# Softmax(scores) @ v on one core: dropping the own-engine waits of the exps and of the copies of transposed tiles

## The chip, the cores and the metric

The kernel runs on one core of one Trainium2 chip. The metric is device time in microseconds (us), taken as the median of several executions of a kernel. Times of profiled executions ("spans") are quoted beside it where a trace is read; they are a little shorter than the measured time.

A core has separate engines that run their own instruction streams: TensorE (PE for its matmuls, PEld for its weight loads), VectorE (DVE), ScalarE (ACT), GpSimd (POOL) and SyncE (SP), and DMA queues that move data. They tell each other of progress through semaphores: counters that instructions step up when they finish, and that other instructions wait on.

## The reference, cut to what matters

```python
scores: (8, 12, 1024, 1024) float32      # 96 heads, 402 MB
v:      (8, 12, 1024, 64)   float32
attn = exp(scores - max)                 # row by row
attn = attn / (sum(attn) + 1e-8)
out  = attn @ v                          # (8, 12, 1024, 64) float32
```

## The kernel before

Four heads are worked on in one iteration of a hardware loop of 24 iterations. One head has R = 8 "rows"; here a row is a tile of 128 rows of scores, 128x1024. For each row ScalarE computes exp into fp16 (mostly two rows in one instruction), TensorE transposes it in C = 8 pieces of 128x128 into PSUM, VectorE copies the transposed row to SBUF, and, two rows later (LAG = 2), TensorE multiplies it with v in 8 matmuls. v has a column of ones, so that the row sums come along. At the end of a head VectorE takes reciprocals and multiplies (`normalise`). The kernel takes exp of the scores as they are: it neither subtracts the maximum nor adds 1e-8.

```python
def heads(n0):
    for k in range(AHEAD):                        # AHEAD = 4 heads
        ...
        for r in range(R):
            if r % EB == 0:                       # EB = 2
                p_nat = take(p_bufs)              # 8 buffers, in turn
                ...
                    nc.scalar.activation(out=p_nat[...], in_=s_bufs[k][...], func=EXP)   # cut
            p_row = p_nat[:, r % EB, :].rearrange(...)
            psT = take(psT_bufs)                  # 4 buffers
            for c in range(C):
                nc.tensor.transpose(out=psT[:, c*P:(c+1)*P], in_=p_row[...], identity=order16[:])
            pt = take(pt_bufs)                    # 4 buffers
            copy = nc.vector.tensor_copy(out=pt[:], in_=psT[:])
            ...
            pending.append((n0, k, r, pt, st))
            if len(pending) > LAG:
                finish(pending.pop(0))            # 8 product matmuls that read pt
    while pending:
        finish(pending.pop(0))
    last(n0)                                      # loads and stores of the iteration's end
...
with tc.For_i(0, BH, AHEAD, iteration_sync="reg_based") as n0:
    queued.clear()
    heads(n0)
```

The framework orders every access to a buffer by semaphores. A copy into `pt` waits for PE, since the product that read the buffer's old content must be done and the new transposes must have landed. It also waits on VectorE's own counter, since the same buffer was written by VectorE four copies earlier. The same holds for an exp, with ScalarE's own counter.

The softmax here doesn't subtract the row's maximum and nothing guards it: scores larger than these inputs give would overflow.

Of the kernel before, what the change touches and what calls it, by code (L numbers as in the profile page):

```python
# [14 lines left out]
def kernel(  # L15
# [6 lines left out]
    nc = tc.nc  # L22
# [69 lines left out]
    def take(bufs):  # L92
        k = turn.get(id(bufs), 0)
        turn[id(bufs)] = k + 1
        return bufs[k % len(bufs)]
# [22 lines left out]
    def normalise(k, st, first, last, behind=None):  # L118

        psO = psO_whole if k % 2 == 0 else psO_banks[first]  # L120
        psO = psO[:, :, 0 : G * M].rearrange("p b (g m) -> p b g m", m=M)
        recip = st["recip"][:, first:last]
        inverse = nc.vector.reciprocal(out=recip, in_=psO[:, :, :, D : D + 1])  # L123
        if behind is not None:
            after(inverse, behind)
        h = k % T
        for t in range(T):
            part = slice(t * W, (t + 1) * W)
            rows = st["out_sb"][h * W : (h + 1) * W, t, first * G : last * G, :]
            nc.vector.tensor_tensor(  # L130
                out=rows.rearrange("j (b g) d -> j b g d", g=G),
                in0=psO[part, :, :, 0:D],
                in1=recip[part].to_broadcast([W, last - first, G, D]),
                op=mybir.AluOpType.mult,
            )

    def finish(u):

        n0, k, r, pt, st = u
        b, g = r // G, r % G  # L140
        if r == 0:
            st["recip"] = take(rc_bufs)
            st["out_sb"] = out_bufs[k // T]
        bank = psO_whole[:, b] if k % 2 == 0 else psO_banks[b][:, 0]
        for c in range(C):
            nc.tensor.matmul(  # L146
                out=bank[:, g * M : (g + 1) * M],
                lhsT=pt[:, c * P : (c + 1) * P],
                rhs=st["vones"][:, c, 0:M],
                start=(c == 0),  # L150
                stop=(c == C - 1),
            )
        if k % 2 == 1:
            if g == G - 1 and (b > 0 or k < AHEAD - 1):
                normalise(k, st, b, b + 1)
        elif r == R - 1:
            normalise(k, st, 0, R // G)
        if r == R - 1:
            spread_v(k)
            if k == T - 1:  # L160
                store(n0, 0)

    def store(n0, k, parts=1):

        rows = out_bh.rearrange("(m x) y -> m x y", x=P)
        size = T * R * D // parts
        for part in range(0, T * R * D, size):
            dma = nc.sync.dma_start(
                out=rows[bass.ds((n0 + k) // T, 1)].rearrange("o x y -> (o x) y")[
                    :, part : part + size  # L170
                ],
                in_=out_bufs[k // T][:].rearrange("x t r d -> x (t r d)")[:, part : part + size],
            )
            for other in stores:
                apart(dma, other)
                apart(other, dma)
            apart(dma, dma)
            stores.append(dma)
            queue(dma)

    stores = []

    def apart(dma, other):
        tc.declare_no_dep(
            dma.ins, other.ins, across_iterations=True, reason="stores of two heads are disjoint"
        )

    def load(k, n, parts=(R,), r=0, **cond):
        for rows in parts:
# [29 lines left out]
    def load_next(k, n0):  # L219

        if k < AHEAD - 2:
            load(k, (n0 + (AHEAD + k)) % BH, cond=n0 < BH - AHEAD)

    def last(n0):


        before = queued[-1:]

        with tc.If(n0 < BH - 2 * AHEAD) as cmp:  # L229
            queued[:] = before  # L230
            load(AHEAD - 2, (n0 + (2 * AHEAD - 2)) % BH)
            load_v((n0 + 2 * AHEAD) % BH)
            load(AHEAD - 1, (n0 + (2 * AHEAD - 1)) % BH)
            store(n0, AHEAD - T)
        with cmp.Else():
            with tc.If(n0 < BH - AHEAD) as cmp2:
                queued[:] = before
                load(AHEAD - 2, BH - 2, (4, 4))
                load(AHEAD - 1, BH - 1, (3,))
                store(n0, AHEAD - T)  # L240
                load(AHEAD - 1, BH - 1, (2, 1, 1, 1), 3)
            with cmp2.Else():
                queued[:] = before
                store(n0, AHEAD - T, T)

    def heads(n0):

        for k in range(AHEAD):
            st = dict(vones=vones_bufs[k])
            for r in range(R):  # L250
                if r % EB == 0:
                    p_nat = take(p_bufs)
                    rows = 1 if k == AHEAD - 1 and r > 0 else EB
                    for g in range(0, EB, rows):
                        nc.scalar.activation(  # L255
                            out=p_nat[:, g : g + rows, :].rearrange(
                                "p r (x v) -> p x r v", v=Q * L
                            ),
                            in_=s_bufs[k][:, r + g : r + g + rows, :].rearrange(
                                "p r (i x l) -> p x (r i) l", i=Q, l=L  # L260
                            ),
                            func=EXP,
                        )
                p_row = p_nat[:, r % EB, :].rearrange("p (h q l) -> p h l q", q=P, l=L)
                psT = take(psT_bufs)
                for c in range(C):
                    nc.tensor.transpose(  # L267
                        out=psT[:, c * P : (c + 1) * P],
                        in_=p_row[:, c // L, c % L, :],
                        identity=order16[:],  # L270
                    )
                pt = take(pt_bufs)
                copy = nc.vector.tensor_copy(out=pt[:], in_=psT[:])  # L273
                if k == AHEAD - 1 and r == R - 1:

                    normalise(k, st, 0, 1, copy)
                if r == R - 1:
                    load_next(k, n0)
# [5 lines that stand above are left out]
        last(n0)  # L284
# [8 lines left out]
# [3 lines that stand above are left out]
# [30 lines left out]
```

## Time and profile before

| | before |
|---|---|
| time, median of three runs | 1063.8 us (1063.76 to 1064.1) |
| profiled span | 1062.3 us |
| instructions | 33,094 |
| busiest engine | ACT, 70% of the span |
| DMA | share of 1.00 in every full loop period, some 432 GB/s |
| after the last landing of scores (1052.0 us) | 10.2 us |

The table says that the kernel is bound by its transfers: no engine is busy all the time, the DMA queues are. Only the last 10 us, in which the last rows are computed and stored, depend on the engines. The lines behind this stand in the prediction below. Two more lines matter for what follows, groups of the page (line, engine, operation, output and input with shapes, count; then busy us and mean ns of one; then the engine's idle time before them and what ended most of it); L255 are the exps, L273 the copies (the transposes are L267, the product is L146).

```profile
L255 ACT ACTIVATE p_nat<-s_nat 128x2048 f16<-128x2048 f32 (+1 forms) x456 | 709.4, 1630 | 219.1 <-DMA s_nat<-in_scores_dram 192.3
...
L273 DVE COPY pt<-psT 128x1024 f16<-128x1024 f16 x768 | 518.1, 689 | 367.1 <-PE L146 134.9
```

VectorE idles 367 us before its copies, and what ended this idle time is PE, not VectorE.

### The profile page before, as it was taken

How to read it: one execution, taken by the hardware profiler on the slowest of the kernel's cores; microseconds unless marked ns; L12 is line 12 of the kernel's file. 1: busy time of each engine (PE TensorE's matmuls, PEld its weight loads, DVE VectorE, ACT ScalarE, POOL GpSimd, SP SyncE). 2: the span in 40 equal slices, each digit the busy share in tenths (PEclk: the TensorE clock that was granted, in tenths of full speed). 3: DMA queues.
4: the chain of work that ended last, by engine and by line, in shares of the span. 5: the costliest groups of instructions: out<-in, count | busy, mean ns of one | idle time of the engine just before them, and what ended most of it. 6: DMA issues, size and time to landing. Idle time of an engine off the chain costs nothing.

```text
span 1062.3 us, 33094 instructions
## 1 busy us (share of the span) xinstructions
PE 722.0 (68%) x12288; PEld 676.5 (64%) x12288; DVE 679.9 (64%) x1205; ACT 740.1 (70%) x480; POOL 243.5 (23%) x406
## 2 busy tenths in 40 slices
PE   2765766767766767667576776767677686666776
PEld 2755756666655667666576666766566676665765
DVE  1765756757666666666676666767567576676667
ACT  3766776666767668676685866767666677666686
POOL 3113112131121311212112221132121311203113
PEclk9988888879898787887988878889888788899889
DMA  9999999999999999999999999999999999999996
GB/s 397 430 417 434 428 434 434 432 435 428 434 432 432 427 433 435 434 434 427 433 429 435 428 433 435 426 441 431 431 434 429 430 428 438 434 434 432 426 432 260
DMA packets 25059, 453.05 MB, mean 426 GB/s; under 512 B 2784, under 2 KB 2784, under 8 KB 9440
## 3 DMA queue, kind: packets, MB, share of 16 engines
q1 hardware_dynamic: 25056, 453.00, 99.4%
q8 instruction: 3, 0.05, 0.0%
HBM read 436.21 MB, written 25.17 MB: 434 GB/s over the span
## 4 chain that ended last, share of the span: by engine, by line
DMA 62%; PE 12%; PEld 6%; DVE 5%; ACT 5%; issue 3%; POOL 3%; SPq 1%; POOLq 1%; ACTq 0%; DVEq 0%; PEldq 0%
DMA s_nat<-in_scores_dram 62%; PE psT L267 7%; DVE pt L273 5%; ACT p_nat L255 5%; PE psO L146 3%; POOL vones L212 3%; PEld L267 3%; PEld L146 3%; PE psO_whole L146 1%; SPq L203 1%; SPq L191 0%; POOLq L212 0%; POOLq L229 0%; POOLq L293 0%; POOLq L321 0%
## 5 line engine op out<-in xcount | busy, mean ns | idle before, releaser
L255 ACT ACTIVATE p_nat<-s_nat 128x2048 f16<-128x2048 f32 (+1 forms) x456 | 709.4, 1630 | 219.1 <-DMA s_nat<-in_scores_dram 192.3
L267 PE MATMUL psT<-order,p_nat 128*128 128x128 f16 x6144 | 562.8, 246 | 281.3 <-ACT p_nat L255 280.9
L273 DVE COPY pt<-psT 128x1024 f16<-128x1024 f16 x768 | 518.1, 689 | 367.1 <-PE L146 134.9
L267 PEld LDWEIGHTS <-p_nat 128*128 128x128 f16 x6144 | 445.4, 123 | 303.5 <-ACT p_nat L255 300.8
L212 POOL CAST vones<-v_sb 32x512 f16<-32x512 f32 x400 | 242.8, 607 | 815.3 <-PE L267 440.3
L146 PEld LDWEIGHTS <-pt 128*128 128x128 f16 x6144 | 302.8, 106 | 76.1 <-DVE pt L273 72.0
L146 PE MATMUL psO<-vones,pt 128*128 128x65 f16 x3072 | 177.5, 202 | 41.4 <-DVE pt L273 39.8
L146 PE MATMUL psO_whole<-vones,pt 128*128 128x65 f16 x3072 | 189.7, 209 | 11.6 <-DVE pt L273 11.2
L255 ACT ACT_TABLE_LOAD x24 | 30.8, 1283 | 94.1 <-DMA s_nat<-in_scores_dram 77.4
L130 DVE TENSOR_TENSOR out_sb<-psO,recip 64x256 f32<-64x256 f32 x192 | 81.2, 423 | 6.1
L130 DVE TENSOR_TENSOR out_sb<-psO_whole,recip 64x512 f32<-64x512 f32 x96 | 66.0, 688 | 3.0
L123 DVE RECIPROCAL recip<-psO 128x4 f32<-128x4 f32 x96 | 16.8, 175 | 0.8
L123 DVE RECIPROCAL recip<-psO_whole 128x8 f32<-128x8 f32 x48 | 9.5, 197 | 0.0
L71 DVE MEMSET vones<- 128x16 f16 x4 | 0.2, 72 | 0.8 <-PEq L310 0.8
L62 DVE CAST order<-ident 128x128 f16<-128x128 f32 x1 | 0.2, 227 | 0.4 <-POOL ident masks.py:199 0.4
masks.py:199 POOL TENSOR_SCALAR_AFFINE_SELECT ident<-ident 128x128 f32<-128x128 f32 x1 | 0.3, 292 | 0.1
masks.py:197 POOL MEMSET ident<- 128x128 f32 x1 | 0.2, 204 | 0.3 <-POOLq L310 0.3
L310 POOL MEMSET const-float32-0.0<- 128x1 f32 x1 | 0.1, 98 | 0.3 <-issue 0.3
L310 POOL MEMSET const-bfloat16-1.0<- 128x1 bf16 x1 | 0.1, 100 | 0.0
L310 POOL MEMSET const-uint8-127<- 128x1 uint8 x1 | 0.1, 100 | 0.0
L310 POOL MEMSET const-float32-1.0<- 128x1 f32 x1 | 0.1, 98 | 0.0
## 6 DMA issues: line engine op xcount, KB each, us to landing
s_nat<-in_scores_dram SPq DMA_DIRECT2D x96, 4096.0 KB, 33.0
v_sb<-in_v_dram SPq DMA_DIRECT2D x24, 1024.0 KB, 19.0
out_dram<-out_sb SPq DMA_DIRECT2D x47, 512.0 KB, 27.7
s_nat<-in_scores_dram SPq DMA_DIRECT2D x2, 2048.0 KB, 32.6
s_nat<-in_scores_dram SPq DMA_DIRECT2D x1, 1536.0 KB, 32.2
s_nat<-in_scores_dram SPq DMA_DIRECT2D x3, 512.0 KB, 20.7
s_nat<-in_scores_dram SPq DMA_DIRECT2D x1, 1024.0 KB, 25.4
out_dram<-out_sb SPq DMA_DIRECT2D x2, 256.0 KB, 2.0
```

The costliest lines, as they stand in the source:

```text
L62: nc.vector.tensor_copy(out=order16[:].rearrange("p (t j) -> p t j", t=T), in_=ident32[:].rearrange("p (j t) -> p t j", t=T),)
L71: nc.vector.memset(vo[:, :, D : D + 2], 1.0)
L123: inverse = nc.vector.reciprocal(out=recip, in_=psO[:, :, :, D : D + 1])
L130: nc.vector.tensor_tensor(out=rows.rearrange("j (b g) d -> j b g d", g=G), in0=psO[part, :, :, 0:D], in1=recip[part].to_broadcast([W, last ...
L146: nc.tensor.matmul(out=bank[:, g * M : (g + 1) * M], lhsT=pt[:, c * P : (c + 1) * P], rhs=st["vones"][:, c, 0:M], start=(c == 0), stop=(c ...
L203: nc.sync.dma_start(out=v_sb[:].rearrange("x h s l d -> x (h s l d)"), in_=rows[bass.ds(n // AHEAD, 1)].rearrange("o x y -> (o x) y"),)
L212: nc.gpsimd.tensor_copy(out=vones_bufs[k][s * Q : (s + 1) * Q, :, 0:D].rearrange("i (h l) d -> i h l d", l=L), in_=v_sb[k * Q : (k + 1) * ...
L255: nc.scalar.activation(out=p_nat[:, g : g + rows, :].rearrange("p r (x v) -> p x r v", v=Q * L), in_=s_bufs[k][:, r + g : r + g + rows, :] ...
L267: nc.tensor.transpose(out=psT[:, c * P : (c + 1) * P], in_=p_row[:, c // L, c % L, :], identity=order16[:],)
L273: copy = nc.vector.tensor_copy(out=pt[:], in_=psT[:])
L310: nc = _bacc.Bacc("TRN2", target_bir_lowering=False, num_devices=1)
```

## The change

Between two writes of the same `pt` buffer there is always PE's product that reads it. The copy waits for that product, and the product waited for the older copy; so the wait on VectorE's own counter is implied. The same goes for exps and transposes. The change declares these write-after-write pairs independent. Its intent is that copies and exps wait for PE (and the loads) alone.

```diff
+    writers = {}
+
+    def apart(a, b, reason="stores of two heads are disjoint"):
+        tc.declare_no_dep(a.ins, b.ins, across_iterations=True, reason=reason)
+
+    def rewrite(buf, op):
+        others = writers.setdefault(buf.name, [])
+        for other in others:
+            apart(op, other, "readers in between")
+            apart(other, op, "readers in between")
+        apart(op, op, "readers in between")
+        others.append(op)
 ... (cut: the old definition of apart goes)
-                        nc.scalar.activation(
+                        exp = nc.scalar.activation(
 ...
+                        rewrite(p_nat, exp)
 ...
                 copy = nc.vector.tensor_copy(out=pt[:], in_=psT[:])
+                rewrite(pt, copy)
```

More of the change, by code (lines that the diff above doesn't have):

```diff
@@ L181 @@
     stores = []
-    def apart(dma, other):
-        tc.declare_no_dep(
-            dma.ins, other.ins, across_iterations=True, reason="stores of two heads are disjoint"
-        )
+    writers = {}
[8 more added lines that the diff above has]
+        others.append(op)
     def load(k, n, parts=(R,), r=0, **cond):
```

## The prediction

> **What bounds the kernel now.** The measured time is 1063.8 us (median of three runs); the profiled span is 1062.3 us. I read the page of the profile first: busy times and slices.
>
> ```profile
> PE 722.0 (68%) x12288; PEld 676.5 (64%) x12288; DVE 679.9 (64%) x1205; ACT 740.1 (70%) x480; POOL 243.5 (23%) x406
> ...
> DMA  9999999999999999999999999999999999999996
> ...
> HBM read 436.21 MB, written 25.17 MB: 434 GB/s over the span
> ```
>
> No compute engine is busy more than 70% of the span, while the DMA row is at its top digit in every slice but the last. To see whether that digit hides idle stretches I cut the loop into its periods (24 iterations of four heads; the exps of the first head of an iteration start every 43.7 us) and asked for the table of stretches. Columns: stretch, length, busy time and count of PE, PEld, DVE, ACT, POOL, granted clock, DMA share, GB/s.
>
> ```profile
> 834.70:878.40 43.70, 31.28 (x512) 29.46 (x512) 28.34 (x50) 30.86 (x21) 9.71 (x16) 0.81 1.00 432
> 878.40:922.00 43.60, 30.23 (x512) 28.60 (x512) 28.41 (x50) 30.83 (x20) 9.71 (x16) 0.84 1.00 432
> 922.00:965.70 43.70, 29.52 (x512) 27.39 (x512) 28.43 (x50) 30.84 (x20) 9.71 (x16) 0.88 1.00 432
> 965.70:1009.40 43.70, 30.39 (x512) 28.66 (x512) 28.29 (x50) 30.83 (x20) 9.71 (x16) 0.84 1.01 433
> 1009.40:1051.50 42.10, 33.04 (x592) 30.89 (x593) 30.75 (x55) 36.71 (x26) 11.07 (x19) 0.88 0.95 406
> 1051.50:1062.30 10.80, 3.60 (x66) 2.83 (x64) 6.12 (x13) 1.80 (x2) 3.51 (x6) 0.88 0.25 97
> ```
>
> Every full period has DMA share 1.00 or 1.01 at 431 to 433 GB/s, whatever the granted clock (0.81 to 0.88) and PE busy time (29.5 to 31.3 us) are. An iteration moves 4 heads of 4 MiB of scores, 1 MiB of v and two stores of 0.5 MiB: 18.87 MB, and 18.87 MB / 432 GB/s = 43.7 us. So from 3 us (first transfer) to 1052 us (last landing of scores) the time is bytes over rate, and every engine has some 13 us of slack per 43.7 us. Only the last 10 us are set by something else.
>
> The chain of waits agrees; its first lines by engine and by line are 62% DMA, the rest small and scattered.
>
> ```profile
> DMA 62%; PE 12%; PEld 6%; DVE 5%; ACT 5%; issue 3%; POOL 3%; SPq 1%; POOLq 1%; ACTq 0%; DVEq 0%; PEldq 0%
> ```
>
> Last, the timeline of VectorE at the end (start, length, instruction, idle before it and who ended it):
>
> ```profile
> 1047.50 0.69 DVE L273 COPY pt<-psT 128x1024 f16<-128x1024 f16 x1 [0.27 <-PE L267]
> 1048.52 0.69 DVE L273 COPY pt<-psT 128x1024 f16<-128x1024 f16 x1 [0.33 <-PE psT L267]
> 1049.42 0.69 DVE L273 COPY pt<-psT 128x1024 f16<-128x1024 f16 x1 [0.21 <-PE L146]
> ...
> 1051.11 1.41 DVE L130 TENSOR_TENSOR out_sb<-psO_whole,recip 64x512 f32<-64x512 f32 x2
> 1052.54 2.48 DVE L273 COPY pt<-psT 128x1024 f16<-128x1024 f16 x4
> 1055.18 0.69 DVE L273 COPY pt<-psT 128x1024 f16<-128x1024 f16 x1 [0.16 <-PE L146]
> ```
>
> Two paces are seen here: single copies 0.90 to 1.02 us apart, and a group of four in 2.48 us, 0.6 us apart. The last copy starts at 1055.18, although the last exp (the records of single instructions: 1052.27 to 1053.30) was done 1.9 us before. VectorE is therefore behind at the very end.
>
> **What the Trainium skill says.** "DMA: Bandwidth & Descriptors", section "Where 436 GB/s comes from", puts the ceiling of a core's DMA ports at 435.2 GB/s; the trace's 431 to 433 GB/s per period agrees, and leaves under 1% to be had in the loop. "Perfetto Trace Analysis", section "Identifying Dependency Chains", says that an instruction that waits on several engines may have separate EventSemaphore instructions placed before it. The trace agrees: the view of the copies' line lists, on VectorE's sequencer,
>
> ```profile
> L273 DVEq EVENT_SEMAPHORE  x480: 21/21/21, 2.1 to 1054.3; - x160
> L273 DVEq FUSED_REGOPS  x456: 46/46/46, 21.1 to 1054.2; - x152
> L273 DVEq ALU_OP  x288: 40/40/40, 31.4 to 1052.3; - x144
> ```
>
> so 480 of 768 copies (20 of the 32 in an iteration) have one, and the program shows that it is the wait on VectorE's own counter; the other 12 have an own wait already implied by a reciprocal's or multiply's. "VectorE: DVE Perf Modes", section "The DRAIN you can't avoid", says of a chain of copies that "the semaphore costs nothing extra here". This trace does not agree as it stands: over all pairs of neighbouring copies, the idle time between them has a median of 0.27 us in the 354 pairs with a wait instruction of the sequencer in between, and is slightly negative (-0.04 us, an overlap) in the 198 without. What makes the 0.27 us I cannot tell from the trace: the wait itself takes 21 ns and is executed 0.11 us after the previous copy starts, well before it ends.
>
> **The change part by part.**
> - Copies: the own-engine wait of 20 copies an iteration goes, so they become what the other 12 are: one register operation and one copy that waits on PE. By the two paces the cost of a copy in a burst goes from 0.96 us (0.69 + 0.27) to about 0.62 us, 0.33 us less. At most 20 x 0.33 = 6.6 us of VectorE time an iteration, 158 us over 24. All of this lies in periods where VectorE has 43.7 - 28.4 = 15 us idle beside the DMA queue: worth 0 there.
> - Exps: 16 of 19 exps an iteration wait on ScalarE's own counter. In the records, exps that follow each other closely overlap by 0.09 us, with or without a wait instruction in between. So this part saves nothing on ScalarE; instructions merely disappear from its sequencer (552 waits now; the own wait mostly sits on the exp itself, and PE's wait will move there). In the last iteration, too, exps are paced by their busy time and the landings: rows 3 to 7 of the last head run back to back from 1048.45, each 0.95 us after the one before, and the last row's data land at 1052.04.
> - The end: ScalarE's last exp ends at 1053.30 in either kernel. With copies at 0.62 us VectorE no longer lags: a head costs it 8 x 0.62 + about 2.0 us for the normalisation = 7.0 us, against 7.3 us of exps. Then: exp of the last row ends 1053.30, transposes 0.65 us (eight matmuls in 0.64 us in this stretch) to 1053.95, copy to 1054.65 instead of 1055.87. What follows (reciprocal, two multiplies of 0.43 us, the same again, store, landing 2.0 us after issue, teardown) has the same length as before. That is 1.2 us earlier. PE's last matmuls and the POOL casts behind them move by the same amount.
>
> Sum: 0 in the start, 0 in 23 periods, 0 for the exps, -1.2 us at the end: 1063.8 - 1.2 = 1062.6 us.
>
> **Rivals.**
> - *Nothing moves at all* (1063.8 us). For it: the order of PE's work, the four transposed buffers and the multiply of the third head at 1051.1 may hold the last copies back just as long; the profile names PE as what ends the gaps before the copies. Against it: in the bursts the transposes had been done up to 0.9 us before the copy that needed them.
> - *The loop gets faster* (by up to 0.7%, to some 1056 us, if each period came down from 432 to 435 GB/s). For it: exps end earlier behind faster copies, so buffers of scores come free earlier. Against it: the share is already 1.00 in every period, and ScalarE waits for landings, not the other way round (192 us of its idle time ended by the loads of scores). More requests waiting in a full queue bring nothing.
> - *It gets slower.* Faster bursts on PE could lower the granted clock (0.86 on average now), or a semaphore wait takes the place of the removed one: PE's wait moves onto the copy or exp itself. Against it: no engine bounds the loop; a 10% longer burst stays inside 13 us of slack. At most the last 10 us grow, by perhaps 0.5 us: 1064.3 us.
> - *The end gains more* (1061.5 us): if the last exps also start earlier. They hang on landings 1.2 us apart (0.5 MB each at 430 GB/s), so at most 0.2 us.
>
> **Range and chances.** The sure part is that the transfers keep 1049 us of the span; what is open is 0 to 2 us at the end, and runs agree within 0.35 us. I take 1062.6, with 1061.4 to 1063.9. A 2% change would be 21 us, twice the whole part of the span that is not transfer-bound, so: faster 0.01, same 0.98, slower 0.01.
>
> **What would show it.** In the changed kernel: the copies' line has no EVENT_SEMAPHORE any more (480 now); copies in bursts 0.6 us apart and the group of gaps of 0.27 us gone; VectorE's busy time unchanged at 680 us; exps as long and as close as before; each period still 43.7 us at 432 GB/s; the last landing of scores at 1052; the last copy within 0.8 us of the last exp's end, and the end of the last multiply near 1056.8 instead of 1058.0. I would be wrong in the main point if a period were shorter than 43.5 us or DMA shares fell under 0.98; wrong in the small one if the 0.27 us gaps stay (then they belong to something else than the removed wait) or if the last copy still starts 1.9 us after the last exp.

## The result, and the profile after

The changed kernel gives the right result and takes 1063.81 us (median of 6 runs, 1063.62 to 1064.31); the kernel before took 1064.01 us on the same chip (6 runs, 1063.76 to 1064.28). The ratio is 0.9999, with a 95% interval of 0.9986 to 1.0012: the same. A ratio in this document is the mean time of one kernel's fast runs over that of the other's of the same rounds, so it is not quite the ratio of the medians quoted. The measured time lies inside the predicted range, but that range reached up to the time of the kernel before, so this says nothing for the mechanism: the predicted gain of 1.2 us is not there.

The page of the changed kernel, first lines (busy times by engine; the DMA row; bytes; the chain of waits by engine):

```profile
span 1061.9 us, 32301 instructions
...
PE 725.7 (68%) x12288; PEld 681.0 (64%) x12288; DVE 680.7 (64%) x1205; ACT 740.3 (70%) x480; POOL 244.5 (23%) x406
...
DMA  9999999999999999999999999999999999999996
...
DMA 62%; PE 15%; ACT 5%; DVE 5%; issue 3%; PEld 3%; POOL 3%; SPq 1%; POOLq 1%; ACTq 0%
```

There are 793 instructions fewer. The DMA row is the same, and busy times are within 0.7%. The groups of exps and copies (now L264 and L283) have nearly the same busy time and idle time as before:

```profile
L264 ACT ACTIVATE p_nat<-s_nat 128x2048 f16<-128x2048 f32 (+1 forms) x456 | 709.5, 1630 | 218.8 <-DMA s_nat<-in_scores_dram 187.4
...
L283 DVE COPY pt<-psT 128x1024 f16<-128x1024 f16 x768 | 518.9, 690 | 366.0 <-PE L146 149.1
```

The table of stretches, with columns as in the prediction, shows that a loop period still has 43.7 us at 432 GB/s:

```profile
834.70:878.40 43.70, 29.86 (x512) 28.01 (x512) 28.24 (x50) 30.88 (x21) 9.75 (x16) 0.84 1.00 432
```

The view of the copies' line shows that the wait instructions are gone. VectorE's sequencer now has one register operation (ALU_OP) for nearly every copy and no EVENT_SEMAPHORE, of which there were 480:

```profile
L283 DVE COPY pt<-psT x768: 679/692/696, 21.2 to 1054.9; 128x1024 f16<-128x1024 f16 x192
L283 DVEq ALU_OP  x744: 40/40/58, 21.2 to 1054.0; - x186
```

Yet the timeline of VectorE at the end is what it was, to within 0.24 us:

```profile
1047.27 0.69 DVE L283 COPY pt<-psT 128x1024 f16<-128x1024 f16 x1 [0.27 <-PE L277]
1048.29 0.69 DVE L283 COPY pt<-psT 128x1024 f16<-128x1024 f16 x1 [0.33 <-PE L146]
1049.19 0.69 DVE L283 COPY pt<-psT 128x1024 f16<-128x1024 f16 x1 [0.21 <-PE L146]
...
1050.87 1.41 DVE L130 TENSOR_TENSOR out_sb<-psO_whole,recip 64x512 f32<-64x512 f32 x2
1052.31 2.49 DVE L283 COPY pt<-psT 128x1024 f16<-128x1024 f16 x4
1054.95 0.69 DVE L283 COPY pt<-psT 128x1024 f16<-128x1024 f16 x1 [0.15 <-PE L146]
```

The gaps of 0.27, 0.33 and 0.21 us are all there, without any wait instruction to make them. The last copy starts 1.7 us after the last exp's end (1053.28), where the prediction allowed 0.8. Over the whole trace, the start-to-start distance of neighbouring copies has its largest cluster at 0.96 us in both kernels: 233 pairs before, 228 after. And the 354 pairs of neighbouring copies that had an own wait between them before are a median of 0.27 us apart in both kernels. So the pace of 0.96 us does not come from the own-engine wait. Something paces the copies at 0.96 us, and the profile calls it PE.

What is odd is that PE is faster than that. In the kernel before, VectorE and PE in one stretch of the loop:

```profile
898.35 0.69 DVE L273 COPY pt<-psT 128x1024 f16<-128x1024 f16 x1 [0.27 <-PE psT L267]
899.31 0.69 DVE L273 COPY pt<-psT 128x1024 f16<-128x1024 f16 x1 [0.27 <-PE L146]
900.27 0.69 DVE L273 COPY pt<-psT 128x1024 f16<-128x1024 f16 x1 [0.27 <-PE psO_whole L146]
```

```profile
898.70 0.61 PE L267 MATMUL psT<-order,p_nat 128*128 128x128 f16 x8
899.15 0.42 PE L146 MATMUL psO_whole<-vones,pt 128*128 128x65 f16 x8
900.97 0.64 PE L267 MATMUL psT<-order,p_nat 128*128 128x128 f16 x8 [1.40 <-ACT p_nat L255]
```

PE starts its rows here 0.70 to 0.81 us apart (transposes at 896.46, 897.16, 897.97 and 898.70), and 0.71 us apart where nothing holds it up (1005.44, 1006.15 and 1006.86). It is idle from 899.57 to 900.97. (In the first rows of a burst PE takes 1.29 us a row, and there its counter keeps up.) All transposes before this were over by 899.32, but the copy at 900.27 is said to wait for PE.

The records of the semaphores in the trace resolve this. Each weight load and each matmul of the loop steps one counter by 1 (the compiled loop body has 512 weight loads and 512 matmuls, each with such a step: 32 a row), and the counter takes its steps one at a time:

```
PE's counter, before: 24,579 records of a step; 22,643 intervals between them are 30 ns
              after:  24,579 records of a step; 22,573 intervals between them are 30 ns
before, 896.04 to 900.72 us: a step every 30 ns or so (no interval over 35 ns); next pause 900.72 to 901.09
PE's last matmul before the pause ended at 899.57
copies that start 0.96 us after the one before: 233 before, 228 after;
  each of them starts 22 to 24 ns after the step that counts the last transpose of its row
  (the transposes themselves had ended a median of 0.55 us earlier before, 0.56 us after)
```

32 steps of 30 ns are 0.96 us. PE's counter thus needs 0.96 us for a row that PE itself does in 0.71 us. In a burst it falls behind, here by 1.15 us, and a copy waits for the number on the counter, not for the matmul. The last copy, too, starts 23 ns after its step in both kernels.

### The profile page after: what moved, and what is told of

Its sections match the earlier page's. It is cut to its first block, busy times and chain, and to the rows that moved or that the text cites. A ratio compares the mean times of both kernels' runs of the same rounds, so it can differ in the third digit from the quotient of the medians.

```text
span 1061.9 us, 32301 instructions
## 1 busy us (share of the span) xinstructions
PE 725.7 (68%) x12288; PEld 681.0 (64%) x12288; DVE 680.7 (64%) x1205; ACT 740.3 (70%) x480; POOL 244.5 (23%) x406
## 4 chain that ended last, share of the span: by engine, by line
DMA 62%; PE 15%; ACT 5%; DVE 5%; issue 3%; PEld 3%; POOL 3%; SPq 1%; POOLq 1%; ACTq 0%
DMA s_nat<-in_scores_dram 62%; PE psT L277 10%; ACT p_nat L264 5%; DVE pt L283 5%; PE psO L146 4%; POOL vones L221 3%; PE psO_whole L146 2%; PEld L277 2%; PEld L146 2%; SPq L212 1%; SPq L200 0%; POOLq L221 0%; POOLq L238 0%; POOLq L304 0%; POOLq L332 0%
## 5 line engine op out<-in xcount | busy, mean ns | idle before, releaser
L264 ACT ACTIVATE p_nat<-s_nat 128x2048 f16<-128x2048 f32 (+1 forms) x456 | 709.5, 1630 | 218.8 <-DMA s_nat<-in_scores_dram 187.4
L283 DVE COPY pt<-psT 128x1024 f16<-128x1024 f16 x768 | 518.9, 690 | 366.0 <-PE L146 149.1
```

The source lines that it names most:

```text
L264: exp = nc.scalar.activation(out=p_nat[:, g : g + rows, :].rearrange("p r (x v) -> p x r v", v=Q * L), in_=s_bufs[k][:, r + g : r + g + ro ...
```

## The experiments

**Theory A**: the 0.27 us belong to PE's counter; the pace of a burst is steps per row times 30 ns. **Theory B**: VectorE has a gap of its own between copies. **Theory C**, named in the expectations: waits on a register's value are slow on VectorE. A further possibility is the prediction's own: the own-engine wait does cost something, and another wait took over its time when it went. The kernel before ran beside each group on the same chip: 1064.16 us median in the first group (7 runs, 1063.84 to 1064.74; e1 to e4), 1063.93 us in the second (9 runs, 1063.57 to 1064.95; e5 to e8). e3, e4 and e7 have a single run each, whose state is therefore unknown; their verdicts rest on distances in the trace, and their granted clocks (0.82, 0.87, 0.84) lie around that of the changed kernel (0.85).

### e1_unrolled: the loop written out, so that PE steps its counter rarely

In straight code the compiler folds PE's steps: 888 matmuls step the counter in the whole program, instead of 24,576 weight loads and matmuls. The conditional loads become Python ifs.

```diff
-    with tc.For_i(0, BH, AHEAD, iteration_sync="reg_based") as n0:
+    for n0 in range(0, BH, AHEAD):
 ... (cut: the conditional loads)
```

> The changed kernel with its loop of 24 iterations written out as straight code; correct result. Outside a loop the compiler folds the steps of PE's counter: 888 counting matmuls in place of 24576 counting instructions (one step per group of 8, by 8, 16 or 24 at once). Theory A (PE's counter takes 30 ns a step, 32 steps a row, so no copy can follow the one before by less than 0.96 us once PE has run ahead): the cluster of copies 0.96 us apart is gone, copies in bursts come 0.60 to 0.75 us apart (busy time 0.69 us overlapping, or PE's 0.71 us a row), the last copy starts within 0.9 us of the last exp's end (1.9 us in both loop kernels), and from the last landing of scores to the end 1.0 to 1.5 us less. Theory B (VectorE itself needs 0.27 us between two copies that read PSUM): 0.96 us stays. Theory C (waits on a register's value are slow on VectorE): gone as well, since waits here are on constants. The whole time is open: straight code may have to be fetched; without that cost 1062.6 us, if its 1.7 MB come through the same DMA engines about 1066.5 us.

Measured: right result, 1080.25 us (1079.88 to 1080.33), ratio 1.015 (1.0133 to 1.0167). The cluster of copies is at 0.70 us (191 pairs) and the one at 0.96 us is gone, as A said. The end was a miss: the last copy starts at 1072.39, 3.9 us after the last exp. The framework had also reordered PE's work (24 transposes in a row, products grouped), so that this run does not settle the end; e5 mends it. The straight code is slower for another reason, told at e5.

### e2_unrolled_before: the same with the own-engine waits kept

```diff
     def rewrite(buf, op):
+        return
 ... (cut: the old body goes; the loop as in e1)
```

> The kernel before (own waits kept), written out as straight code in the same way, with folded steps of PE's counter; correct result. It repeats the change where the counter is no longer in the way. Theory A with own waits that cost nothing (they are long met): copies 0.60 to 0.75 us apart as in e1, time within 0.3 us of e1. If own waits did cost the 0.27 us after all and something else hid their removal in the loop: copies 0.96 us apart here and not in e1, and the time about 1.2 us above e1.

Measured: right result, 1080.47 us (1080.16 to 1081.07), ratio 1.0154 (1.0138 to 1.0171), the same as e1. Neighbouring copies with an own wait instruction in between are a median of 14 ns apart, those without 162 ns. If the own wait cost 0.27 us, the first number could not be this small. Its order of work is again not the kernel's own, so e6 repeats it.

### e3_fewer_steps: half of the product's matmuls

The result is wrong: 24 steps a row instead of 32, so A wants 24 x 30 ns = 0.72 us.

```diff
-        for c in range(C):
+        for c in range(C // 2):
...
-                stop=(c == C - 1),
+                stop=(c == C // 2 - 1),
```

> The changed kernel, loop kept, with only 4 of the 8 matmuls of a row's product (half of the keys): wrong result on purpose. 24 steps of PE's counter a row. Theory A: the cluster of copies at 0.96 us moves to 0.72 us (24 x 30 ns), and the last copy follows the last exp by under 1.0 us. Theories B and C: the cluster stays at 0.96 us. Time 1062.3 to 1063 us by A, 1063.5 to 1063.8 us by B and C; the period of the loop 43.7 us by all.

Measured: 1062.99 us in one run, 1.2 us under the median of the kernel before on the same chip. The cluster at 0.96 us has 19 pairs left; the clusters are 0.72 us (56 pairs) and VectorE's own pace of 0.60 and 0.61 us (153 and 122). The end of VectorE's timeline:

```profile
1051.06 2.04 DVE L283 COPY pt<-psT 128x1024 f16<-128x1024 f16 x3
1053.60 1.41 DVE L283 COPY pt<-psT 128x1024 f16<-128x1024 f16 x2 [0.50 <-PE psO L146]
```

The last copy starts at 1054.32, 0.77 us after the last exp (1053.54): the lag that the prediction wanted from the change comes here, from fewer steps. PE also had less work in this run, so it alone does not separate the counter from PE's work; e4 does that better.

### e4_more_steps: eight steps a row more, with next to no work

Four matmuls of one column a row go to unused columns of PSUM: 4 weight loads and 4 matmuls, 40 steps a row. A wants 1.20 us. The result stays right.

```diff
+        for c in range(4):
+            nc.tensor.matmul(
+                out=bank[:, 500 + c : 501 + c],
+                lhsT=pt[:, c * P : (c + 1) * P],
+                rhs=st["vones"][:, c, 0:1],
+                start=True,
+                stop=True,
+            )
```

> The changed kernel, loop kept, with 4 small extra matmuls a row (one column each, into unused PSUM columns); correct result. 40 steps of PE's counter a row. Theory A: the cluster of copies moves from 0.96 to 1.20 us (40 x 30 ns). Theories B and C: it stays at 0.96 us, since PE's own time a row goes from 0.71 us to about 0.9 us at most. The loop's period stays 43.7 us by all (32 rows x 1.20 us = 38.4 us fit). At the end by A the backlog since about 1029 us grows by 0.24 us a row for about 26 rows: the time rises by 3 to 6 us, to 1067 to 1070 us; by B and C under 1 us.

Measured: right result, 1072.05 us in one run, 7.9 us more than the kernel before. VectorE near the end:

```profile
1052.13 0.69 DVE L291 COPY pt<-psT 128x1024 f16<-128x1024 f16 x1 [0.51 <-PE L154]
1053.33 0.69 DVE L291 COPY pt<-psT 128x1024 f16<-128x1024 f16 x1 [0.51 <-PE L154]
```

The copies are exactly 1.20 us apart; the cluster at 1.20 us has 336 pairs, and 29,486 of the counter's 30,722 intervals are 30 ns. The loop is unmoved, as before by the transfers:

```profile
834.70:878.40 43.70, 33.66 (x640) 31.61 (x640) 29.13 (x50) 30.84 (x20) 9.71 (x16) 0.88 1.00 432
```

PE's busy time in the period grew by 3.8 us against the changed kernel (granted clock 0.88 and 0.84), 0.12 us a row, which would bring PE's 0.71 us to 0.83 us by estimate, not to 1.20. The transposes of the two copies shown had ended 1.6 and 1.7 us before they start, and both start 24 ns after their step. So the steps are the pace. Theory C falls here and in e3: both keep the waits on registers, and the pace moved with the steps. The time was mis-sized: 3 to 6 us were expected. The counter steps without a break from 1029.31 to 1065.07 us, as expected from about 1029, but for 1,192 steps, 30 rows and not 26. It took 35.8 us for these rows, where the changed kernel took 29.2 us, and it reached them 2.1 us later (1027.16 in the changed kernel). Why it came later was not looked for.

### e5_ordered_after and e6_ordered_before: straight code in the kernel's own order of work

As e1 and e2, with PE's work kept in the order in which the kernel writes it. PE then steps its counter once per transposed row (768 steps) and 120 times for products.

```diff
+    with tc.manual_schedule(engines={mybir.EngineType.PE}):
+        for n0 in range(0, BH, AHEAD):
+            heads(n0)
 ... (cut: the loop's own line goes; the conditional loads as in e1)
```

> The changed kernel as straight code again, but with PE's instructions held in the order of the loop (e1 let the scheduler move whole groups of transposes ahead, which spoilt its end); PE's counter is folded to one step per transposed row. Correct result. Theory A (the counter's steps, 30 ns each, set the pace of copies): no cluster at 0.96 us, copies in bursts 0.60 to 0.75 us apart, last copy starts within 0.9 us of the last exp's end (1.9 and 1.7 us in the loop kernels, 3.9 us in e1), and from the landing of the last row of scores to the end 8.6 to 9.2 us, against 10.2 and 9.9 us in the loop kernels. Theory B (0.27 us of VectorE's own after each copy): 0.96 us and 9.9 us stay. Whole time: as e1, 1078 to 1081 us, since what e1 lost it lost before its end.

> As e5 with the own waits of the kernel before kept; correct result. It asks what an own wait costs where PE's counter no longer hides it. Theory A, own waits free: within 0.3 us of e5, copies as close as there. If own waits cost what the prediction gave them: copies 0.3 us further apart than in e5, last copy 1 us or more later after the last exp, time about 1.2 us above e5.

Measured, both with the right result: e5 1077.18 us (1077.08 to 1077.6), ratio 1.0124 (1.0108 to 1.0139); e6 1077.51 us (1077.15 to 1077.86), ratio 1.0127 (1.0112 to 1.0143). The clusters of e5 are at 0.60, 0.61, 0.70 and 0.71 us, with 3 pairs at 0.96. Its last two copies:

```profile
1068.59 0.69 DVE L277 COPY pt<-psT 128x1024 f16<-128x1024 f16 x1 [0.26 <-PE psT L271]
1069.53 0.69 DVE L277 COPY pt<-psT 128x1024 f16<-128x1024 f16 x1 [0.25 <-PE psT L271]
```

The last exp ends at 1068.80, so the last copy starts 0.73 us after it: the predicted 0.8 us. In e6, with the own waits kept, it is 0.73 us as well (1068.75 and 1069.48), and copies are a median of 16 ns apart with an own wait instruction in between (288 pairs). The same 288 pairs in e5, which has no such wait, are a median of 15 ns apart. So with the counter out of the way, the own wait is worth next to nothing, and nothing at the end: the prediction's reading of the own wait falls. The two medians differ by 0.33 us, but the intervals overlap. The ends of PE's records are modelled, so one might think that PE itself needs 0.96 us a row and the records hide it; e5 and e6 have the same PE instructions in the kernel's order of work, and copies follow each other there at 0.60 to 0.71 us.

From the last landing of scores to the end there are 7.9 us in both, where 10.2 and 9.9 us are in the loop kernels. Below the expected 8.6 to 9.2 us; I did not follow that up. The gain is spent many times over: the last landing of scores is at 1067.56 us, 15.5 us later than in the loop kernels. The page shows one thing that the straight code moves in addition, against 0.07 MB in the changed kernel:

```profile
q8 instruction: 96, 1.57, 0.5%
```

1.5 MB more at some 430 GB/s would be 3.5 us by estimate; by the page's share, 0.5% of the span, 5.4 us. Another part is lost late: from 1053.2 to 1067.5 us the DMA share is only 0.56 (230 GB/s). What keeps the queues from being full there is not explained by any run here.

### e7_half_copy: a copy of half the size

The copy takes 512 of 1024 columns (the result is wrong; VectorE clears the `pt` buffers once at the start). If VectorE had a gap of its own, the gap would stay and the distance would shrink; if PE's counter paces, the distance stays and the gap grows.

```diff
-                copy = nc.vector.tensor_copy(out=pt[:], in_=psT[:])
+                copy = nc.vector.tensor_copy(out=pt[:, 0 : SK // 2], in_=psT[:, 0 : SK // 2])
 ... (cut: the clearing of pt)
```

> The changed kernel, loop kept, copying only the first 512 of 1024 columns of a transposed row: wrong result on purpose. A copy takes about 0.42 us in place of 0.69 us. Theory A: the cluster of copies stays at 0.96 us from start to start, the idle time between them grows from 0.27 to about 0.54 us. Theory B: the idle time stays 0.27 us and the cluster moves to about 0.69 us. Time 1063.2 to 1064 us by A; about 1062.6 us by B.

Measured: 1063.93 us in one run.

```profile
1053.44 0.42 DVE L285 COPY pt<-psT 128x512 f16<-128x512 f16 x1 [0.54 <-PE L279]
1054.40 0.42 DVE L285 COPY pt<-psT 128x512 f16<-128x512 f16 x1 [0.53 <-PE L279]
```

A copy takes 0.42 us instead of 0.69, and the distance stays at 0.96 us (190 pairs): the gap has grown from 0.27 to 0.54 us. Theory B falls.

### e8_lag3: the product one row later

If copies are held back by the steps of products written between two transposes, more distance might let the last copies go earlier.

```diff
-    LAG = 2
+    LAG = 3
```

> The changed kernel, loop kept, with the products three rows behind the transposes instead of two (LAG = 3); correct result, the same instructions. By theory A the counter has 16 fewer steps (0.48 us) to make before it reaches a row's transposes, so at the end the last copy starts 0.3 to 0.5 us earlier after the last exp; the last product's steps come later by as much as they were moved. Time 1063.3 to 1063.8 us, a gain of 0.2 to 0.5 us at best. Theories B and C: no change (within 0.2 us).

Measured: right result, 1063.85 us (1063.63 to 1064.28), ratio 0.9998 (0.9984 to 1.0011): the same. The cluster at 0.96 us fell to 77 pairs and 112 are at 0.61, but the last copy starts at 1055.15, 1.8 us after the last exp (1053.34).

```profile
1051.80 1.41 DVE L130 TENSOR_TENSOR out_sb<-psO_whole,recip 64x512 f32<-64x512 f32 x2
1053.23 2.61 DVE L283 COPY pt<-psT 128x1024 f16<-128x1024 f16 x4
```

The third head's multiply now comes about 0.9 us later (1051.80 instead of 1050.87), and four copies queue behind it. The last copy starts 0.26 us after its step this time, held up by VectorE's own queue. The counter still has the same number of steps to make, and makes the last 898 of them without a break (1029.87 to 1056.81). The run shows that the lag is no remedy.

No version was found that beats both kernels. Fewer steps with the loop kept and a right result would be wanted; no run has that. By e3, a single run with less PE work as well, it might bring some 1 us of 1064.

## Why the prediction was right or wrong, point by point

- **The bound: right.** (One detail was misread: the exps at the edges of its stretches, seven instructions from 1009.42 us, are those of an iteration's last head, not its first. The period is the same.) The table of stretches shows transfers at a share of 1.00 in every full period of both kernels, and even e4, with 1.20 us a row, leaves the period at 43.7 us. "0 in 23 periods" held.
- **The exps: right.** Busy time of 709.4 and 709.5 us, the same landings, last exp's end at 1053.30 and 1053.28.
- **The instructions: right.** The copies' EVENT_SEMAPHORE are gone, VectorE's busy time has stayed (679.9 and 680.7 us).
- **The pace of copies: this step failed.** It read "the cost of a copy in a burst goes from 0.96 us (0.69 + 0.27) to about 0.62 us". It stayed at 0.96 us, since 0.96 us is what PE's counter takes for the 32 steps of a row. Shown by three doses in the same loop, 24, 32 and 40 steps giving 0.72, 0.96 and 1.20 us; by the copies at these paces, which start 22 to 24 ns after their step; by e7, where a shorter copy left the distance as it was; and by e5 and e6, where the 0.96 us vanished with and without the own wait.
- **What led me to it.** I had compared the gaps of pairs with and without an own wait instruction, 0.27 us against -0.04 us, and taken the correlation for a cause. The 12 copies of an iteration without an own wait are each among the first three after a multiply, because the multiply's own wait already implies theirs; and during the multiplies PE's counter goes on, so that the next copies find their number already there. Both come from the multiply. The changed kernel shows it: its copies have no own wait at all, and the same two groups of pairs are still 0.27 us and -0.07 us apart. The profile had named PE as what ended these gaps, which I set aside since the transposes "had been done up to 0.9 us before the copy that needed them". They had been done, but not counted.
- **The end: failed with it.** "That is 1.2 us earlier" rested on the pace alone. Measured: the last copy starts 0.23 us earlier (1055.18 to 1054.95), and the profiled spans differ by 0.3 us (1062.26 and 1061.93), while the medians differ by 0.2 us, inside the spread of either kernel's runs. In both kernels PE's counter makes its last 622 steps without a break, at 30 ns each, from 1037.94 to 1056.60 us before and from 1037.70 to 1056.37 after; the last copy waits for a step inside this stretch. The 0.23 us by which the last copy is earlier were there at the start of this stretch; what made them was not looked for, and runs of one kernel differ by more. What the removed wait would have been worth can be seen in e5 against e6: nothing that their intervals separate.
- **The rival "Nothing moves at all": right**, and for the reason given there, that the profile names PE. Its other reasons (the four buffers, the multiply of the third head) were not what did it: the last copy starts 23 ns after its step. The order of PE's work matters only in that it sets how many steps come before a row's last one.
- **The skill.** "VectorE: DVE Perf Modes", section "The DRAIN you can't avoid", says of a chain of copies that "the semaphore costs nothing extra here". The prediction set it aside; e6 and e5 agree with it, with 16 and 15 ns between the same copies with and without the wait. "TensorE: Matmul & The Clock Gate", section "The cost: per-tile semaphore tail", says that steps of a semaphore at the end of matmuls serialise, with a fitted 26.3 ns for each. I did not look there, as the change touches no TensorE instruction. 32 steps at that figure would be an estimate of 0.84 us, above PE's 0.71 us for a row; the trace has 30 ns a step, and 0.96 us.

## What to carry to other kernels

A gap that the profile puts down to an engine which had long been idle may be that engine's counter: count the steps per unit of work, multiply by the interval seen in the semaphore records, and compare with the engine's own pace, before you credit the gap to a wait on the waiting side. When two groups differ in the thing you want to remove, ask what else they differ in (here, the multiply in front of them) before taking the difference as its price. And where transfers bound the loop, a change to waits can only pay in the last microseconds, where it has to move whatever paces the end.

## What the Trainium skill lacked or had wrong

- "TensorE: Matmul & The Clock Gate", section "The cost: per-tile semaphore tail": the cost is told as a tail after packed tiles, 26.3 ns a step. The runs show 30 ns a step, that weight loads step as well, and that it limits a running pipeline: 24, 32 and 40 steps a row give copies 0.72, 0.96 and 1.20 us apart, where PE's work takes 0.71 us.
- "Perfetto Trace Analysis", section "Identifying Dependency Chains": it does not say that the counter can lag behind its engine. The page lists the propagation of a semaphore among what the profile hides, but not that steps queue up. In the kernel before the counter went on stepping until 900.72, 1.15 us after PE's last matmul.
- "VectorE: DVE Perf Modes", section "The DRAIN you can't avoid": not wrong; e6 and e5 confirm it for copies of 128x1024 in fp16, with a median of 16 ns from one to the next across an own wait and 15 ns for the same copies without it.
- "Runtime: NRT & Kernel Launch", section "Instruction fetch mechanics", takes the fetching of long code to be mostly hidden, and does not say what it takes from the DMA engines: 1.57 MB and 0.5% of their time in e5, against 0.07 MB in the loop. The last landing of scores came 15.5 us later (1067.56 instead of 1052.0), of which the runs trace only a part to this.
